# Sliding-window gather on one core: whole 16 KB output rows from two partition halves, with loads of 8 partitions from SyncE and GpSimd

## The chip, the cores and the metric

The kernel runs on one core of one Trainium2 chip. The time is the device time of that core in microseconds (us), the median of several executions. The span of a profiled execution is the time from its first to its last instruction; the time is some 1.7 us longer than the span. Engines are named TensorE (PE), VectorE (DVE), ScalarE (ACT), GpSimd (POOL) and SyncE (SP). The profile counts 16 DMA engines for the core, and all queues share them: from 100 to 160 us 16.2 packets of all queues together are in flight on average before. "The packet records" are the trace's list of every DMA packet with its queue, start, duration and size; they do not name the engine.

## The reference, cut to what matters

```python
batch, c, h, w = (16, 64, 64, 64)          # float32
window_size, stride = 8, 4                 # 15 x 15 windows
for i in range(n_h):
    for j in range(n_w):
        result[:, i, j] = x[:, :, i*4 : i*4+8, j*4 : j*4+8]
# result: (16, 15, 15, 64, 8, 8)
```

There is no arithmetic. Every input row is read once, each inner pixel is written four times: 16.78 MB in, 58.98 MB out.

## The kernel before

Partition = image x channel half x quarter of the rows. Each partition holds 32 channels of 16 image rows, so it can fill four window rows ("slots") of any column of windows; the last slot needs 4 rows of the next quarter, which a shuffle by one partition brings. One window in the output is 16 KB for all channels, so one partition writes 8 KB of it.

```python
L = lpool.tile([P, CL, RB, W], f32)                       # 128 x (32 x 16 x 64)
for k in (2, 0, 1, 3):                                    # quarters of the channels
    for q in range(HQ):
        (nc.sync, nc.scalar)[q % 2].dma_start(out=L[q::HQ, k*cw:(k+1)*cw], in_=x_v[q, :, k*cw:(k+1)*cw, :])
# ... 11 small instructions make the row numbers of the scatters ...
def window(j, s, half):                                   # half: 16 of the 32 channels, or None
    if not last:
        nc.scalar.copy(out=g, in_=L[:, cs, s*ST : s*ST+WS, cols])
    else:
        nc.vector.tensor_copy(out=g[:, :, 0:ST, :], in_=L[:, cs, s*ST:RB, cols])
        nc.vector.stream_shuffle(out=g[:, :, ST:WS, :], in_=L[:, cs, 0:ST, cols], mask=nxt)
    # the last two windows: stores from SyncE; all others: one scatter from GpSimd
    nc.gpsimd.indirect_dma_start(out=o, out_offset=..., in_=g, ...)
# ... the first 8 windows are filled and stored by halves of the channels,
# so that stores are queued before the last quarter of the loads is in ...
```

Of the kernel before, what the change touches and what calls it, by code (L numbers as in the profile page):

```python
# [1 line left out]

# [4 lines left out]


@with_exitstack  # L10
def kernel(
    ctx: ExitStack,
    tc: tile.TileContext,
    x: bass.AP,
    window_size: int,
    stride: int,
    out: bass.AP,
):
    nc = tc.nc
    P = nc.NUM_PARTITIONS  # L20

    B, C, H, W = x.shape
    Bo, NH, NW, Co, WSo, WSo2 = out.shape
    WS = int(window_size)
    ST = int(stride)
    assert Bo == B and Co == C and WSo == WS and WSo2 == WS

    f32 = mybir.dt.float32
    i32 = mybir.dt.int32
    ALU = mybir.AluOpType  # L30
    HQ = 4
    CH = P // (B * HQ)
    CL = C // CH
    RB = H // HQ
    NSLOT = RB // ST
    NWIN = NH * NW
    CFREE = CL * WS * WS
    assert HQ == 4 and CH == 2 and WS == 2 * ST

    lpool = ctx.enter_context(tc.tile_pool(name="lpool", bufs=1))  # L40
    ipool = ctx.enter_context(tc.tile_pool(name="ipool", bufs=1))
    gpool = ctx.enter_context(tc.tile_pool(name="gpool", bufs=1))


    L = lpool.tile([P, CL, RB, W], f32)
    x_v = x.rearrange("b (ch cl) (hq r) w -> hq (b ch) cl (r w)", ch=CH, hq=HQ)
    NCH = 4
    cw = CL // NCH

    for k in (2, 0, 1, 3):  # L50
        for q in range(HQ):
            (nc.sync, nc.scalar)[q % 2].dma_start(
                out=L[q::HQ, k * cw : (k + 1) * cw, :, :],
                in_=x_v[q, :, k * cw : (k + 1) * cw, :],
            )


    def itile(name):
        return ipool.tile([P, 1], i32, name=name)

    pi, tb, tq, tc_, idx, idx_last = (itile(n) for n in ("pi", "tb", "tq", "tc", "idx", "idx_last"))
    nc.gpsimd.iota(pi[:, :], pattern=[[0, 1]], base=0, channel_multiplier=1)  # L62
    nc.vector.tensor_scalar(out=tb[:, :], in0=pi[:, :], scalar1=3, scalar2=None, op0=ALU.logical_shift_right)  # L63
    nc.vector.tensor_scalar(out=tc_[:, :], in0=pi[:, :], scalar1=2, scalar2=1, op0=ALU.logical_shift_right, op1=ALU.bitwise_and)  # L64
    nc.vector.tensor_scalar(out=tq[:, :], in0=pi[:, :], scalar1=HQ - 1, scalar2=None, op0=ALU.bitwise_and)  # L65
    nc.vector.tensor_scalar(out=tb[:, :], in0=tb[:, :], scalar1=float(NWIN * CH), scalar2=None, op0=ALU.mult)  # L66
    nc.vector.tensor_tensor(out=tb[:, :], in0=tb[:, :], in1=tc_[:, :], op=ALU.add)  # L67
    nc.vector.tensor_scalar(out=tc_[:, :], in0=tq[:, :], scalar1=float(NSLOT * NW * CH), scalar2=None, op0=ALU.mult)  # L68
    nc.vector.tensor_tensor(out=idx[:, :], in0=tb[:, :], in1=tc_[:, :], op=ALU.add)  # L69

    nc.vector.tensor_scalar(out=tq[:, :], in0=tq[:, :], scalar1=float(HQ - 1), scalar2=float(2 * B * NWIN * CH), op0=ALU.is_equal, op1=ALU.mult)  # L71
    nc.vector.tensor_tensor(out=idx_last[:, :], in0=idx[:, :], in1=tq[:, :], op=ALU.add)  # L72


    HCL = CL // 2
    idx_h, idx_hlast = itile("idx_h"), itile("idx_hlast")
    for d, e in ((idx_h, idx), (idx_hlast, idx_last)):
        nc.vector.tensor_scalar(out=d[:, :], in0=e[:, :], scalar1=2.0, scalar2=None, op0=ALU.mult)  # L78
    o_v = out.rearrange("b i j (ch cl) r w -> (b i j ch) (cl r w)", ch=CH)
    o_h = out.rearrange("b i j (ch cl) r w -> (b i j ch) (cl r w)", ch=2 * CH)  # L80
    nxt = [min(p + 1, 31) for p in range(32)]

    order = [(j, s) for j in range(NW) for s in range(NSLOT)]


    TAIL, BACK = 2, 3
    o_q = out.rearrange("b i j (ch cl) r w -> i j b ch (cl r w)", ch=CH)

    def free(st):
        tc.declare_no_dep(st.ins, group="stores", reason="each store writes rows of its own")  # L90
        tc.add_to_no_dep_group("stores", st.ins)


    UNITS = 18
    G = [gpool.tile([P, 2 * HCL, WS, WS], f32, name=f"G{n}") for n in range(UNITS // 2)]
    at = 0

    def window(j, s, half):
        nonlocal at
        cols = slice(j * ST, j * ST + WS)  # L100
        last = s == NSLOT - 1
        if half is None:
            n, c0 = 2, 0
            at += at % 2
        else:
            n, c0 = 1, half * HCL
        u = at % UNITS
        at += n
        cs = slice(c0, c0 + n * HCL)
        g = G[u // 2][:, u % 2 * HCL : (u % 2 + n) * HCL, :, :]  # L110
        if not last:
            nc.scalar.copy(out=g, in_=L[:, cs, s * ST : s * ST + WS, cols])  # L112
        else:
            nc.vector.tensor_copy(out=g[:, :, 0:ST, :], in_=L[:, cs, s * ST : RB, cols])  # L114
            nc.vector.stream_shuffle(out=g[:, :, ST:WS, :], in_=L[:, cs, 0:ST, cols], mask=nxt)  # L115
        if (j, s) in order[-TAIL:]:
            g_q = g.rearrange("(m q) c r w -> q m (c r w)", q=HQ)
            for q in range(HQ - 1 if last else HQ):
                free(nc.sync.dma_start(out=o_q[q * NSLOT + s, j], in_=g_q[q]))
            return  # L120
        if half is None:
            o, ix = o_v, (idx_last if last else idx)
        else:
            o, ix = o_h, (idx_hlast if last else idx_h)
        st = nc.gpsimd.indirect_dma_start(  # L125
            out=o,
            out_offset=bass.IndirectOffsetOnAxis(ap=ix[:, 0:1], axis=0),
            in_=g.rearrange("p c r w -> p (c r w)"),
            in_offset=None,
            element_offset=(s * NW + j) * CH * CFREE + (half or 0) * HCL * WS * WS,  # L130
            bounds_check=B * NWIN * CH * (1 if half is None else 2) - 1,
            oob_is_err=False,
        )
        free(st)

    EARLY = 8
    for j, s in order[:EARLY]:
        window(j, s, 0)
    late = list(order[:EARLY])
    rest = list(order[EARLY:])  # L140
    while late:
        for w in late[:2]:
            window(*w, 1)
        for w in rest[:2]:
            window(*w, None)
        late, rest = late[2:], rest[2:]
    for w in rest[:-TAIL]:
        window(*w, None)
    at -= 2 * BACK
    for w in rest[-TAIL:]:  # L150
        window(*w, None)


# [1 line left out]
_INS = ['x', 'window_size', 'stride']  # L155
_OUTS = [((16, 15, 15, 64, 8, 8), 'float32')]

_NUMBERS = {'window_size': 8, 'stride': 4}


# [26 lines left out]
```

## Time and profile before

| | before |
|---|---|
| time, median (lowest to highest) | 193.51 us (193.43 to 193.98) |
| span of the profiled execution | 191.9 us |
| ScalarE / VectorE / GpSimd busy | 45% / 16% / 34% |
| DMA, middle of the run | 405 to 430 GB/s in each slice, no gap |
| scatters, bytes in one | 66, 8 KB a partition (16 of them 4 KB) |

The lines that carry this stand in the prediction below. Read them so: the digits of the DMA row are tenths of the 16 engines' time, one digit a fortieth of the span; if all are 9, only bytes, rate and the two ends can change the time. A compute engine's "idle before, releaser" then tells only that it waits for buffers.

### The profile page before, as it was taken

The numbers are of one execution on the slowest core, as the hardware profiler recorded it, in microseconds if no ns is written. First come the engines' busy times: TensorE is split into PE (matmuls) and PEld (weight loads), VectorE is DVE, ScalarE is ACT, GpSimd is POOL, SyncE is SP. The second block draws the span as 40 slices with busy tenths as digits, with TensorE's granted clock in tenths as the row PEclk, the third lists the DMA queues.
The fourth block names the chain that finished last, engine by engine and source line by source line (L and its number), as shares of the span: only waits on it lengthen the run. The fifth ranks groups of instructions, "written<-read, shape, count | busy, mean of one in ns | idle before, by whom it ended". The sixth has DMA issues, their size and how long they took to land.

```text
span 191.9 us, 458 instructions
## 1 busy us (share of the span) xinstructions
DVE 30.3 (16%) x62; ACT 86.2 (45%) x52; POOL 64.4 (34%) x71
## 2 busy tenths in 40 slices
DVE  2000000402322121211103120303030303000030
ACT  0000000495999646565655656474747473300300
POOL 0000000177877754543434344444444444400000
DMA  5999999999999999999999999999999999999785
GB/s 175 419 412 410 410 410 410 410 410 419 420 430 418 424 415 405 413 412 415 417 418 413 410 412 410 408 406 410 412 413 405 408 405 408 415 413 417 307 277 179
DMA packets 14196, 75.80 MB, mean 395 GB/s; under 512 B 1936, under 2 KB 1936, under 8 KB 7952
## 3 DMA queue, kind: packets, MB, share of 16 engines
q0 software_dynamic: 9504, 57.15, 73.1%
q1 hardware_dynamic: 2512, 10.22, 13.8%
q10 hardware_dynamic: 2176, 8.39, 11.1%
q14 instruction: 4, 0.03, 0.0%
HBM read 16.78 MB, written 62.65 MB: 414 GB/s over the span
## 4 chain that ended last, share of the span: by engine, by line
DMA 66%; issue 25%; POOL 3%; DVE 1%; POOLq 0%; DVEq 0%; PEldq 0%
DMA out_dram<-G,idx 56%; DMA out_dram<-G,idx_h 9%; POOL out_dram L125 3%; DVE G L115 1%; DVE G L114 0%; POOLq L125 0%; POOL pi L62 0%; DVEq L114 0%; PEldq L182 0%
## 5 line engine op out<-in xcount | busy, mean ns | idle before, releaser
L112 ACT COPY G<-L 128x2048 f32<-128x2048 f32 (+1 forms) x51 | 85.0, 1696 | 59.2 <-DMA out_dram<-G,idx_last 25.0
L125 POOL DMA_INDIRECT out_dram<-G,idx x38 | 36.8, 969 | 49.5 <-DMA out_dram<-G,idx 45.6
L114 DVE COPY G<-L 128x1024 f32<-128x1024 f32 (+1 forms) x17 | 11.0, 646 | 152.8 <-DMA out_dram<-G,idx 88.4
L115 DVE STREAM_SHUFFLE G<-L 128x1024 f32<-128x1024 f32 (+1 forms) x17 | 19.5, 1146 | 0.0
L112 ACT ACT_TABLE_LOAD x1 | 1.3, 1283 | 36.3 <-DMA L<-in_x_dram 36.3
L125 POOL DMA_INDIRECT out_dram<-G,idx_hlast x4 | 4.0, 1001 | 37.7 <-DVE G L115 36.8
L125 POOL DMA_INDIRECT out_dram<-G,idx_last x12 | 11.6, 963 | 11.7 <-DVE G L115 7.8
L125 POOL DMA_INDIRECT out_dram<-G,idx_h x12 | 11.7, 975 | 3.7 <-issue 2.4
L63 DVE TENSOR_SCALAR tb<-pi 128x1 int32<-128x1 int32 x1 | 0.2, 153 | 1.0 <-POOL pi L62 1.0
L62 POOL IOTA pi<- 128x1 int32 x1 | 0.1, 119 | 0.4 <-PEq L182 0.4
L115 DVE LOAD_MASK_SELECT G<-L x17 | 0.2, 13 | 0.0
L168 POOL MEMSET const-float32-0.0<- 128x1 f32 x1 | 0.1, 98 | 0.2 <-issue 0.2
L69 DVE CUSTOM_DVE_ANT_0 idx<-tb,tc 128x2 uint16<-128x2 uint16 x1 | 0.2, 161 | 0.0
L67 DVE CUSTOM_DVE_ANT_0 tb<-tb,tc 128x2 uint16<-128x2 uint16 x1 | 0.2, 159 | 0.0
L68 DVE TENSOR_SCALAR tc<-tq 128x1 int32<-128x1 int32 x1 | 0.2, 154 | 0.0
L78 DVE TENSOR_SCALAR idx_hlast<-idx_last 128x1 int32<-128x1 int32 x1 | 0.2, 153 | 0.0
L78 DVE TENSOR_SCALAR idx_h<-idx 128x1 int32<-128x1 int32 x1 | 0.2, 154 | 0.0
L72 DVE CUSTOM_DVE_ANT_0 idx_last<-idx,tq 128x2 uint16<-128x2 uint16 x1 | 0.1, 150 | 0.0
L66 DVE TENSOR_SCALAR tb<-tb 128x1 int32<-128x1 int32 x1 | 0.1, 149 | 0.0
L71 DVE TENSOR_SCALAR tq<-tq 128x1 int32<-128x1 int32 x1 | 0.1, 147 | 0.0
L64 DVE TENSOR_SCALAR tc<-pi 128x1 int32<-128x1 int32 x1 | 0.1, 144 | 0.0
L65 DVE TENSOR_SCALAR tq<-pi 128x1 int32<-128x1 int32 x1 | 0.1, 143 | 0.0
(3 smaller groups left out, 0.3 us busy)
## 6 DMA issues: line engine op xcount, KB each, us to landing
L<-in_x_dram ACTq DMA_DIRECT2D x8, 1024.0 KB, 19.8
L<-in_x_dram SPq DMA_DIRECT2D x8, 1024.0 KB, 20.1
out_dram<-G SPq DMA_DIRECT2D x7, 256.0 KB, 4.1
out_dram<-G,idx POOLq DMA_INDIRECT x38, 18.8
out_dram<-G,idx_h POOLq DMA_INDIRECT x12, 7.0
out_dram<-G,idx_last POOLq DMA_INDIRECT x12, 18.8
out_dram<-G,idx_hlast POOLq DMA_INDIRECT x4, 8.0
```

The source lines that it names most:

```text
L62: nc.gpsimd.iota(pi[:, :], pattern=[[0, 1]], base=0, channel_multiplier=1)
L63: nc.vector.tensor_scalar(out=tb[:, :], in0=pi[:, :], scalar1=3, scalar2=None, op0=ALU.logical_shift_right)
L64: nc.vector.tensor_scalar(out=tc_[:, :], in0=pi[:, :], scalar1=2, scalar2=1, op0=ALU.logical_shift_right, op1=ALU.bitwise_and)
L65: nc.vector.tensor_scalar(out=tq[:, :], in0=pi[:, :], scalar1=HQ - 1, scalar2=None, op0=ALU.bitwise_and)
L67: nc.vector.tensor_tensor(out=tb[:, :], in0=tb[:, :], in1=tc_[:, :], op=ALU.add)
L68: nc.vector.tensor_scalar(out=tc_[:, :], in0=tq[:, :], scalar1=float(NSLOT * NW * CH), scalar2=None, op0=ALU.mult)
L69: nc.vector.tensor_tensor(out=idx[:, :], in0=tb[:, :], in1=tc_[:, :], op=ALU.add)
L78: nc.vector.tensor_scalar(out=d[:, :], in0=e[:, :], scalar1=2.0, scalar2=None, op0=ALU.mult)
L112: nc.scalar.copy(out=g, in_=L[:, cs, s * ST : s * ST + WS, cols])
L114: nc.vector.tensor_copy(out=g[:, :, 0:ST, :], in_=L[:, cs, s * ST : RB, cols])
L115: nc.vector.stream_shuffle(out=g[:, :, ST:WS, :], in_=L[:, cs, 0:ST, cols], mask=nxt)
L125: st = nc.gpsimd.indirect_dma_start(out=o, out_offset=bass.IndirectOffsetOnAxis(ap=ix[:, 0:1], axis=0), in_=g.rearrange("p c r w -> p (c r ...
```

## The change

Its intent: let each store packet be a whole 16 KB row, so that the fixed cost of a packet and of a scatter (4 ns and some 55 ns by the records of before, as the prediction works out) is paid half as often, and let stores begin when half of the images (y = 0) are in. The channel halves move to the two partition halves; the lower 64 partitions collect one slot, the upper 64 the next, and each buffer is filled from both halves by copies that shift by 64 partitions. The loads go by 8 partitions.

```diff
-    HQ = 4
-    CH = P // (B * HQ)
+    CH = 2
+    HQ = P // (B * CH)
...
-    for k in (2, 0, 1, 3):
+    SMALL = 4
+    for y in range(NY):
         for q in range(HQ):
-            (nc.sync, nc.scalar)[q % 2].dma_start(...)          # 32 partitions
+            load(nc.sync, 0, y, q, SMALL, CL)                   # 8 partitions each
+            load(nc.gpsimd, 0, y, q, 0, SMALL)
+            load(nc.gpsimd, 1, y, q, 0, CL)
...
+    for t in range(NG): ...                                     # zero what early scatters drop
+            nc.vector.memset(G[t][p0 : p0 + QP, :, :, :], 0.0)
+    for y in range(NY):                                         # early: columns 0 to 2, slots 0/1
+        for j in range(EARLY):
+            for half in range(CH):
+                fill(G[t % NG], half, half, j, y * QP, QP, (act, dve))
+            scatter(G[t % NG], (idx_y0, idx_y1)[y], j, 0)
...
+        if s == 0:                                              # slots 0 and 1
+            for half in range(CH):
+                fill(g, half, s + half, j, 0, HP, (act, dve))
+            scatter(g, idx, j, s)
+        else:                                                   # slots 2 and 3
+            turn = j % 2
+            fill(g, turn, s, j, 0, HP, (act, act))
+            fill(g, 1 - turn, s + 1, j, 0, HP, (dve, dve))
+            scatter(g, (idx_hi, idx_lo)[turn], j, s)
```

`fill` makes two copies, one from the partitions' own half of the channels and one from the other half. A "unit" below is one buffer's worth: four such copies and the scatter that stores it. The row numbers for the scatters take 21 small instructions on VectorE; they stand after the loads in the program text.

More of the change, by code (lines that the diff above doesn't have):

```diff
@@ L36 @@
     NWIN = NH * NW
-    CFREE = CL * WS * WS
-    assert HQ == 4 and CH == 2 and WS == 2 * ST
+    CFREE = C * WS * WS
+    HP = P // CH
+    YB = 8
+    NY = B // YB
+    QP = YB * HQ
+    assert HQ == 4 and WS == 2 * ST and QP == 32 and NSLOT == 4
     lpool = ctx.enter_context(tc.tile_pool(name="lpool", bufs=1))
@@ L45, with load @@
     L = lpool.tile([P, CL, RB, W], f32)
-    x_v = x.rearrange("b (ch cl) (hq r) w -> hq (b ch) cl (r w)", ch=CH, hq=HQ)
-    NCH = 4
-    cw = CL // NCH
-    for k in (2, 0, 1, 3):
+    x_v = x.rearrange("(y b) (ch cl) (hq r) w -> ch y hq b cl (r w)", y=NY, ch=CH, hq=HQ)
+    SMALL = 4
+    def load(eng, ch, y, q, c0, c1):
+        p0 = ch * HP + y * QP + q
+        eng.dma_start(out=L[p0 : p0 + QP - HQ + 1 : HQ, c0:c1, :, :], in_=x_v[ch, y, q, :, c0:c1, :])
+    for y in range(NY):
         for q in range(HQ):
-            (nc.sync, nc.scalar)[q % 2].dma_start(
-                out=L[q::HQ, k * cw : (k + 1) * cw, :, :],
-                in_=x_v[q, :, k * cw : (k + 1) * cw, :],
-            )
+            load(nc.sync, 0, y, q, SMALL, CL)
+            load(nc.gpsimd, 0, y, q, 0, SMALL)
+            load(nc.gpsimd, 1, y, q, 0, CL)
@@ L58, in itile @@
     def itile(name):
         return ipool.tile([P, 1], i32, name=name)
-    pi, tb, tq, tc_, idx, idx_last = (itile(n) for n in ("pi", "tb", "tq", "tc", "idx", "idx_last"))
+    pi, tb, tq, tc_, th, idx, idx_y0, idx_y1, idx_lo, idx_hi = (
+        itile(n) for n in ("pi", "tb", "tq", "tc", "th", "idx", "idx_y0", "idx_y1", "idx_lo", "idx_hi")
+    )
+    FAR = float(2 * B * NWIN)
     nc.gpsimd.iota(pi[:, :], pattern=[[0, 1]], base=0, channel_multiplier=1)
-    nc.vector.tensor_scalar(out=tb[:, :], in0=pi[:, :], scalar1=3, scalar2=None, op0=ALU.logical_shift_right)
@@ L64 @@
-    nc.vector.tensor_scalar(out=tc_[:, :], in0=pi[:, :], scalar1=2, scalar2=1, op0=ALU.logical_shift_right, op1=ALU.bitwise_and)
-    nc.vector.tensor_scalar(out=tq[:, :], in0=pi[:, :], scalar1=HQ - 1, scalar2=None, op0=ALU.bitwise_and)
-    nc.vector.tensor_scalar(out=tb[:, :], in0=tb[:, :], scalar1=float(NWIN * CH), scalar2=None, op0=ALU.mult)
-    nc.vector.tensor_tensor(out=tb[:, :], in0=tb[:, :], in1=tc_[:, :], op=ALU.add)
-    nc.vector.tensor_scalar(out=tc_[:, :], in0=tq[:, :], scalar1=float(NSLOT * NW * CH), scalar2=None, op0=ALU.mult)
@@ L69 @@
-    nc.vector.tensor_tensor(out=idx[:, :], in0=tb[:, :], in1=tc_[:, :], op=ALU.add)
-    nc.vector.tensor_scalar(out=tq[:, :], in0=tq[:, :], scalar1=float(HQ - 1), scalar2=float(2 * B * NWIN * CH), op0=ALU.is_equal, op1=ALU.mult)
-    nc.vector.tensor_tensor(out=idx_last[:, :], in0=idx[:, :], in1=tq[:, :], op=ALU.add)
-    HCL = CL // 2
-    idx_h, idx_hlast = itile("idx_h"), itile("idx_hlast")
-    for d, e in ((idx_h, idx), (idx_hlast, idx_last)):
-        nc.vector.tensor_scalar(out=d[:, :], in0=e[:, :], scalar1=2.0, scalar2=None, op0=ALU.mult)
@@ L79 @@
-    o_v = out.rearrange("b i j (ch cl) r w -> (b i j ch) (cl r w)", ch=CH)
-    o_h = out.rearrange("b i j (ch cl) r w -> (b i j ch) (cl r w)", ch=2 * CH)
-    nxt = [min(p + 1, 31) for p in range(32)]
-    order = [(j, s) for j in range(NW) for s in range(NSLOT)]
-    TAIL, BACK = 2, 3
-    o_q = out.rearrange("b i j (ch cl) r w -> i j b ch (cl r w)", ch=CH)
-    def free(st):
-        tc.declare_no_dep(st.ins, group="stores", reason="each store writes rows of its own")
-        tc.add_to_no_dep_group("stores", st.ins)
@@ L94 @@
-    UNITS = 18
-    G = [gpool.tile([P, 2 * HCL, WS, WS], f32, name=f"G{n}") for n in range(UNITS // 2)]
-    at = 0
-    def window(j, s, half):
-        nonlocal at
-        cols = slice(j * ST, j * ST + WS)
-        last = s == NSLOT - 1
-        if half is None:
-            n, c0 = 2, 0
-            at += at % 2
-        else:
-            n, c0 = 1, half * HCL
-        u = at % UNITS
-        at += n
-        cs = slice(c0, c0 + n * HCL)
-        g = G[u // 2][:, u % 2 * HCL : (u % 2 + n) * HCL, :, :]
-        if not last:
-            nc.scalar.copy(out=g, in_=L[:, cs, s * ST : s * ST + WS, cols])
-        else:
-            nc.vector.tensor_copy(out=g[:, :, 0:ST, :], in_=L[:, cs, s * ST : RB, cols])
-            nc.vector.stream_shuffle(out=g[:, :, ST:WS, :], in_=L[:, cs, 0:ST, cols], mask=nxt)
-        if (j, s) in order[-TAIL:]:
-            g_q = g.rearrange("(m q) c r w -> q m (c r w)", q=HQ)
-            for q in range(HQ - 1 if last else HQ):
-                free(nc.sync.dma_start(out=o_q[q * NSLOT + s, j], in_=g_q[q]))
-            return
-        if half is None:
-            o, ix = o_v, (idx_last if last else idx)
-        else:
-            o, ix = o_h, (idx_hlast if last else idx_h)
@@ new lines, in bits, with mul, tt @@
+    def bits(d, shift, mask):
+        nc.vector.tensor_scalar(out=d[:, :], in0=pi[:, :], scalar1=shift, scalar2=mask, op0=ALU.logical_shift_right, op1=ALU.bitwise_and)
+    def mul(d, a, m):
+        nc.vector.tensor_scalar(out=d[:, :], in0=a[:, :], scalar1=float(m), scalar2=None, op0=ALU.mult)
+    def tt(d, a, b, op):
+        nc.vector.tensor_tensor(out=d[:, :], in0=a[:, :], in1=b[:, :], op=op)
+    bits(tb, 2, B - 1)
+    bits(tq, 0, HQ - 1)
+    bits(tc_, 6, 1)
+    mul(tb, tb, NWIN)
+    mul(th, tq, NSLOT * NW)
@@ new lines @@
+    tt(tb, tb, th, ALU.add)
+    mul(th, tc_, NW)
+    tt(idx, tb, th, ALU.add)
+    bits(th, 5, 1)
+    mul(th, th, FAR)
+    tt(idx_y0, idx, th, ALU.add)
+    nc.vector.tensor_scalar(out=th[:, :], in0=th[:, :], scalar1=-1.0, scalar2=FAR, op0=ALU.mult, op1=ALU.add)
+    tt(idx_y1, idx, th, ALU.add)
+    nc.vector.tensor_scalar(out=tq[:, :], in0=tq[:, :], scalar1=float(HQ - 1), scalar2=FAR, op0=ALU.is_equal, op1=ALU.mult)
+    tt(th, tc_, tq, ALU.mult)
+    tt(idx_hi, idx, th, ALU.add)
+    nc.vector.tensor_scalar(out=tc_[:, :], in0=tc_[:, :], scalar1=-1.0, scalar2=1.0, op0=ALU.mult, op1=ALU.add)
@@ L125, in window, with scatter @@
+    tt(th, tc_, tq, ALU.mult)
+    tt(idx_lo, tb, th, ALU.add)
+    mul(th, tc_, NW)
+    tt(idx_lo, idx_lo, th, ALU.add)
+    o_v = out.rearrange("b i j c r w -> (b i j) (c r w)")
+    nxt = [min(p + 1, 31) for p in range(32)]
+    NG = 4
+    G = [gpool.tile([P, C, WS, WS], f32, name=f"G{n}") for n in range(NG)]
+    def scatter(g, ix, j, s):
         st = nc.gpsimd.indirect_dma_start(
-            out=o,
+            out=o_v,
             out_offset=bass.IndirectOffsetOnAxis(ap=ix[:, 0:1], axis=0),
@@ L129, in window @@
             in_offset=None,
-            element_offset=(s * NW + j) * CH * CFREE + (half or 0) * HCL * WS * WS,
-            bounds_check=B * NWIN * CH * (1 if half is None else 2) - 1,
+            element_offset=(s * NW + j) * CFREE,
+            bounds_check=B * NWIN - 1,
             oob_is_err=False,
         )
-        free(st)
-    EARLY = 8
-    for j, s in order[:EARLY]:
-        window(j, s, 0)
-    late = list(order[:EARLY])
-    rest = list(order[EARLY:])
-    while late:
-        for w in late[:2]:
-            window(*w, 1)
-        for w in rest[:2]:
-            window(*w, None)
-        late, rest = late[2:], rest[2:]
@@ L147, with fill @@
-    for w in rest[:-TAIL]:
-        window(*w, None)
-    at -= 2 * BACK
-    for w in rest[-TAIL:]:
-        window(*w, None)
+        tc.declare_no_dep(st.ins, group="stores", reason="each store writes rows of its own")
+        tc.add_to_no_dep_group("stores", st.ins)
+    def fill(g, half, s, j, lo, n, copies):
+        d = slice(half * HP + lo, half * HP + lo + n)
+        cols = slice(j * ST, j * ST + WS)
+        for ch in (half, 1 - half):
+            f = slice(ch * HP + lo, ch * HP + lo + n)
+            cs = slice(ch * CL, (ch + 1) * CL)
+            copy = copies[ch != half]
+            if s < NSLOT - 1:
+                copy(out=g[d, cs, :, :], in_=L[f, :, s * ST : s * ST + WS, cols])
+            else:
+                copy(out=g[d, cs, 0:ST, :], in_=L[f, :, s * ST : RB, cols])
+                nc.vector.stream_shuffle(out=g[d, cs, ST:WS, :], in_=L[f, :, 0:ST, cols], mask=nxt)
@@ new lines @@
+    act, dve = nc.scalar.copy, nc.vector.tensor_copy
+    EARLY = 3
+    assert EARLY < NG
+    for t in range(NG):
+        for half in range(CH):
+            p0 = half * HP + (QP if t < EARLY else 0)
+            nc.vector.memset(G[t][p0 : p0 + QP, :, :, :], 0.0)
+    t = 0
+    for y in range(NY):
[3 more added lines that the diff above has]
+            scatter(G[t % NG], (idx_y0, idx_y1)[y], j, 0)
+            t += 1
@@ new lines @@
+    units = [(j, s) for j in range(NW) for s in (0, 2) if s or j >= EARLY]
+    for j, s in units:
+        g = G[t % NG]
+        t += 1
+        if s == 0:
+            for half in range(CH):
+                fill(g, half, s + half, j, 0, HP, (act, dve))
+            scatter(g, idx, j, s)
+        else:
+            turn = j % 2
+            fill(g, turn, s, j, 0, HP, (act, act))
+            fill(g, 1 - turn, s + 1, j, 0, HP, (dve, dve))
+            scatter(g, (idx_hi, idx_lo)[turn], j, s)
```

## The prediction

> **What bounds the kernel now.** I read the busy shares by engine first, then the row of DMA activity over 40 slices, then the table of stretches, then the groups of instructions by form, and last the chain of waits and the timeline near the end. Shares and slices:
>
> ```profile
> DVE 30.3 (16%) x62; ACT 86.2 (45%) x52; POOL 64.4 (34%) x71
> ...
> DMA  5999999999999999999999999999999999999785
> GB/s 175 419 412 410 410 410 410 410 410 419 420 430 418 424 415 405 413 412 415 417 418 413 410 412 410 408 406 410 412 413 405 408 405 408 415 413 417 307 277 179
> ```
>
> No compute engine is busy even half of the time, and DMA is full in every slice but the first and the last three. The kernel is a copy: 16.78 MB in, and 16 x 15 x 15 x 64 x 64 x 4 bytes = 58.98 MB out, 75.76 MB together. At 410 GB/s that is 184.8 us of a 191.9 us span; the other 7 us are the start and the tail. A slice is 4.8 us, so the first loses (410-175)/410 x 4.8 = 2.8 us and the last three lose (103+133+231)/410 x 4.8 = 5.5 us. The stretches:
>
> ```profile
> 30.00:60.00 30.00, 6.05 (x15) 21.34 (x18) 17.12 (x18) 1.00 1.03 417
> 60.00:90.00 30.00, 5.94 (x9) 19.37 (x11) 16.16 (x17) 1.00 1.02 415
> 90.00:120.00 30.00, 5.68 (x9) 17.07 (x9) 11.56 (x12) 1.00 1.01 412
> ```
>
> Columns: stretch, length, busy time and count of VectorE, ScalarE and GpSimd, clock, DMA share, GB/s. The first has the hand-over from loads to stores in it (loads end near 45 us) and shows no gap: copies of 16 channels, ready when half of a quarter-sliced load is there, put stores in the queues (GpSimd's first at 37.7 us) before the loads run out. That is the thing to keep in mind for the change.
>
> Durations that I shall reuse:
>
> ```profile
> L112 ACT COPY G<-L 128x2048 f32<-128x2048 f32 x39 | 73.8, 1897 | 56.9 <-DMA out_dram<-G,idx_last 25.0 <-DMA out_dram<-G,idx 17.1 <-DVE G L115 13.3
> L125 POOL DMA_INDIRECT out_dram<-G,idx x38 | 36.8, 969 | 49.5 <-DMA out_dram<-G,idx 45.6 <-issue 2.8 <-ACT G L112 1.1
> L115 DVE STREAM_SHUFFLE G<-L 128x1024 f32<-128x1024 f32 x13 | 16.6, 1278 | 0.0
> L114 DVE COPY G<-L 128x1024 f32<-128x1024 f32 x13 | 9.3, 715 | 105.9 <-DMA out_dram<-G,idx 88.4 <-DMA out_dram<-G,idx_h 9.6 <-ACT G L112 7.9
> L114 DVE COPY G<-L 128x512 f32<-128x512 f32 x4 | 1.7, 422 | 46.9 <-DMA L<-in_x_dram 41.4 <-DMA out_dram<-G,idx_h 5.5
> ```
>
> The copies wait for stores (buffers), not the other way round. The tail in the timeline:
>
> ```profile
> 166.62 0.96 POOL L125 DMA_INDIRECT out_dram<-G,idx  x1 [1.73 <-DMA out_dram<-G,idx]
> 179.87 1.90 ACT L112 COPY G<-L 128x2048 f32<-128x2048 f32 x1 [14.74 <-DMA out_dram<-G,idx_last]
> 181.79 5.67 SPq L119 DMA_DIRECT2D out_dram<-G  x7
> ```
>
> The last two windows are filled late and stored from SyncE while the GpSimd queue runs dry. The trace's packet records show why: from 180 to 183 us only 8 of the 16 DMA engines still have store packets; these 8 lag by about 3.5 us. The same records say when they fall behind: in stretches without a scatter being issued an 8 KB packet takes 314 ns on average, in those with one 325 to 335 ns with single ones near 400. 3.5 us over 66 scatters is some 55 ns each. With half the engines idle a packet takes 309 ns, a 4 KB packet 159.
>
> [...]
>
> **The change, part by part.**
>
> *Bytes.* The same 75.76 MB, so a DMA floor of about 184 us stays. All gain must come from time per byte, the start or the tail.
>
> *Row size.* Stores go from 8 KB to 16 KB rows. In the records successive 4 KB packets of an engine start 155 ns apart, 8 KB ones 306: a fixed part of 4 ns. A 16 KB row then costs 608 instead of 612, 0.7%. With all engines working it is 2 x 311 - 4 = 618.
>
> *Scatters.* 66 become 33 (six half ones for 3 columns x 2 image halves, 12 pairs of slots 0/1, 15 pairs of slots 2/3). The lag of the slow engines halves, from 3.5 to about 1.8 us. But the dropped rows now fall on one half of the partitions at a time[...]. Store phase of the lower engines: 226 x 618 = 139.7, plus 33 x 80 ns of lag and completion = 2.6: about 142.3 us.
>
> *Loads.* 16.78 MB. [...]256 packets of 4 KB at 155-160 ns = 40 to 41 us. Starting at 2.2 us (the first load packet of before)[...], they end at 43 to 44.
>
> *Where the early stores go.* The intent is plain: image half y=0 is loaded by about 23 us, its copies fill three buffers, and stores could begin at 25 us. But in the order of instructions as built, VectorE executes 8 memsets, 6 copies for y=0, **two copies that wait for the y=1 loads**, and only then the 21 small index instructions. The first scatter needs the index tile of y=0, the twelfth of these. VectorE is in order, so no scatter leaves before all loads are in. ([...]6 copies of 1.3 us, from 422 and 715 ns extrapolated to 2048 elements, end near 42.6 us: hidden, just.) So at the hand-over: loads end 43.8, semaphore 0.75 (before: last load packet 44.97, VectorE starts 45.74), copies 1.3 to 2.6, twelve index instructions 1.4 (before: eleven from 0.98 to 2.34), GpSimd's start 0.3, first data 1.3 (SyncE's store at the tail: issue 181.79, packet 183.10). First store packet at about 50 us. DMA is **idle for some 6 us** where before had no gap.
>
> *Ramp.* Four half scatters (2.55 us of DMA each) follow 1.27 us apart and end at 60.2. A buffer is refilled by two ScalarE copies of 1.9 us, so ScalarE gives a unit every 3.8 us; the fifth and sixth are in time, the seventh (ready 64.7, data 66.3, queue dry at 65.3) leaves a hole of about 1 us. After that each unit is 4 to 5 us of DMA against 3.8 of ScalarE, or 2 x (0.7 + 1.28) = 4.0 of VectorE, and four 2 MB buffers hold 15 us of pending work. Compute is hidden: ScalarE 66 x 1.9 = 125 us in all.
>
> *Tail.* No queue change at the end; both halves finish together but for about 2 rows (1.2 us, counted), then 1.3 us to the span's end as before (190.59 to 191.9).
>
> Sum: 50 + 142.3 + 1 + 1.3 = 194.6 us of span. The measured time of before is 1.65 over its span (193.55 against 191.9), so 196.2. In differences: tail and lag gain 4 to 5, row size under 1, hand-over loses 6 to 7, ramp 1.
>
> **Rivals.** *A, the early stores work*: no idle hand-over, stores mixed with loads. Then 43 + 142.3 + 2 + 1.3 + 1.65 = about 190. For it speaks that the whole kernel is laid out for it; against it the order on VectorE, which I take as decisive. *B, the 16 KB rows stream distinctly better*, at the 309 ns per 8 KB that half-idle engines show: 226 x 614 + 2.6 = 141.4, one us less; even without lag it gives 193 to 195. A real jump is not to be seen: the stretch with many 4 KB rows (45 to 90 us) ran at 418 GB/s, that with 8 KB rows alone (90 to 178 us) at 411. [...]*D, compute becomes the bound*: [...]in the steady state it needs 6.6 us per two units against 10 of DMA, so only if shifted copies cost half as much again. Then 205.
>
> **Range and chances.** Store phase 139 to 145 and first store at 48 to 53 us span most of the doubt: 191.5 to 201.5. Two per cent are 189.7 and 197.4. Faster needs A and a better rate, 0.06. The upper limit is only 1.2 us above my figure, so slower gets 0.36, the same 0.58.
>
> **What would show it.** Right: a trough in the DMA row at 44 to 50 us, first scatter of GpSimd at 48 to 49 behind VectorE's index instructions, 410 to 420 GB/s after it, and no low slices but the last. Wrong: scatters at 25 us (A), store slices above 425 (B), 200 GB/s during the loads (C), or dips in mid-run with waits of scatters for VectorE or ScalarE (D).

Rival C: loads on half of the engines at half of 410 GB/s, some 80 us, and a time near 235. The 256 packets of the loads are 16.78 MB in packets of 4 KB, shared evenly by 16 engines. The 226 rows of "the lower engines" are 6 x 4 + 12 x 8 + 8 x 8 + 7 x 6 rows, for eight engines that write the partition half with fewer dropped rows; the other eight have 224. That a half falls on eight engines was an assumption. The changed kernel's records bear it out: of the first scatter of slots 2 and 3, which drops 16 rows of one half, 4-byte packets come eight at 72.99, 16 at 74.83 and eight at 76.00 us, 16 for the dropped rows and 16 more, and 1.85 us are three rows of 618 ns. Of the 80 ns for each scatter 55 are the lag worked out above; the rest was my estimate. The 42.6 us have a memset time in them; in rival D "it" is VectorE.

## The result, and the profile after

The changed kernel takes 203.58 us (203.29 to 203.67), the kernel before 193.51. The ratio is 1.0513 (95% interval 1.0493 to 1.0533). Here and below a ratio is the mean time of one kernel's runs over that of the other's of the same rounds, so it isn't quite the ratio of the medians quoted. Executions over 1.5% slower than the fastest of the same kernel are left out of the means. I had forecast 196.2 with a range of 191.5 to 201.5: the direction was within what I allowed, the size was not.

The page of the changed kernel, busy times and the 40 slices (now 5.05 us each):

```profile
DVE 131.2 (65%) x155; ACT 125.5 (62%) x67; POOL 52.6 (26%) x54
...
DMA  2999999993299899999999999999999999999980
GB/s 93 337 406 399 401 399 400 398 397 98 104 409 406 330 390 412 409 422 416 414 416 429 430 416 416 419 416 432 425 419 416 416 422 432 425 419 414 416 373 36
```

The DMA row of this page has a hole that the row of before has not: 98 and 104 GB/s in the two slices from 45 to 56 us. The loads before it run at 400 where before had 410, the stores after it at 414 to 432 where before had 405 to 418, and the slices at both ends are lower. The stretches (columns: stretch, length, busy time and count of VectorE, ScalarE, GpSimd, clock, DMA share, GB/s), first of before, then of after:

```profile
5.00:40.00 35.00, 2.00 (x6) 3.69 (x4) 1.99 (x2) 1.00 1.03 411
90.00:178.00 88.00, 15.19 (x24) 43.63 (x23) 30.82 (x32) 1.00 1.01 411
```

```profile
5.00:45.00 40.00, 31.27 (x14) 12.27 (x7) 7.46 (x12) 1.00 1.03 392
90.00:180.00 90.00, 58.81 (x74) 73.77 (x41) 25.78 (x20) 1.00 1.01 421
```

Loads lost 5% of their rate (in part because GpSimd's begin late, at 5.06 us), stores won 2.4%. By these rates the 58.98 MB of stores gain 143.5 - 140.1 = 3.4 us, and the 16.78 MB of loads lose 42.8 - 40.8 = 2.0.

The hole, in the timeline of after (start, length, engine, what, count, and in brackets how long the engine had waited and for what):

```profile
35.67 6.93 DVE L136 COPY G<-L 32x2048 f32<-32x2048 f32 x6
...
48.04 2.47 DVE L136 COPY G<-L 32x2048 f32<-32x2048 f32 x2 [5.44 <-issue]
50.54 0.15 DVE L77 TENSOR_SCALAR tb<-pi 128x1 int32<-128x1 int32 x1
...
51.93 0.16 DVE L83 CUSTOM_DVE_ANT_0 idx_y<-idx,th 128x2 uint16<-128x2 uint16 x1
...
52.77 0.15 DVE L103 TENSOR_SCALAR tc<-tc 128x1 int32<-128x1 int32 x1
52.95 1.07 POOL L115 DMA_INDIRECT out_dram<-G,idx_y  x1 [16.09 <-DVE tc L103]
```

By 42.6 us VectorE has filled three buffers with rows of y = 0. They are ready to store, but the row numbers come at 52 us: VectorE stops before the two copies for y = 1 (they start at 48.04; the profile names no releaser, but the last load packet has ended at 47.24) and makes its row numbers only after them. GpSimd waited 16 us for them.

The groups of instructions that answer to those shown of before:

```profile
L136 ACT COPY G<-L 64x2048 f32<-64x2048 f32 (+1 forms) x66 | 124.2, 1896 | 28.9 <-DMA out_dram<-G,idx 10.1
L136 DVE COPY G<-L 64x2048 f32<-64x2048 f32 (+1 forms) x36 | 43.9, 1227 | 22.8 <-DMA out_dram<-G,idx 12.7
L139 DVE STREAM_SHUFFLE G<-L 64x1024 f32<-64x1024 f32 x30 | 38.3, 1276 | 0.0
L150 DVE MEMSET G<- 32x4096 f32 x8 | 27.8, 3472 | 8.0 <-issue 5.4
L115 POOL DMA_INDIRECT out_dram<-G,idx x12 | 13.8, 1149 | 34.7 <-ACT G L136 29.2
L115 POOL DMA_INDIRECT out_dram<-G,idx_hi x8 | 11.7, 1459 | 31.1 <-DVE G L139 17.9
```

A copy to shifted partitions costs what an unshifted one of as many elements a partition did (1896 against 1897 ns on ScalarE, whose 66 copies, shifted or not, all take 1888 to 1902), and half-filled lanes (64 of 128 partitions) save nothing. That doubles the copying, and yet compute isn't the bound: the copies still wait for stores.

From the packet records I worked out where DMA engines stood idle: the sum, over the time, of the engines below 16 that have a packet in flight, divided by 16. This gives the ledger of the 9.9 us between the spans:

| us of full DMA lost, or time | before | after | difference |
|---|---|---|---|
| start, 0 to 8 us | 2.44 | 3.90 | +1.46 |
| hand-over from loads to stores, 44 to 56 us | 0.00 | 7.61 | +7.61 |
| ramp after it, 56 to 90 us | 0.01 | 1.76 | +1.75 |
| uneven ends of the engines, from 170 us to the last store packet | 2.84 | 1.77 | -1.07 |
| last store packet to the end of the span | 1.32 | 3.26 | +1.94 |
| the rest, engines working | 185.3 | 183.5 | -1.8 |
| span | 191.9 | 201.8 | +9.9 |

The ramp is the stretch of the first scatters, before the copies have run ahead of the stores. The idea of the change is in the last line but one and is worth 1.8 us net of slower loads; another 1.1 us comes from ends that are less uneven. The other lines are what it costs to start, hand over and end.

### The profile page after: what moved, and what is told of

The parts are those of the page before. It is cut to its first block, busy times and chain, and to the rows that moved or that the text cites. A ratio compares the mean times of both kernels' runs of the same rounds, so it can differ in the third digit from the quotient of the medians.

```text
span 201.8 us, 478 instructions
## 1 busy us (share of the span) xinstructions
DVE 131.2 (65%) x155; ACT 125.5 (62%) x67; POOL 52.6 (26%) x54
## 3 DMA queue, kind: packets, MB, share of 16 engines
HBM read 16.78 MB, written 69.21 MB: 426 GB/s over the span
## 4 chain that ended last, share of the span: by engine, by line
DMA 65%; issue 8%; DVE 7%; ACT 7%; POOL 3%; POOLq 1%; DVEq 0%; PEldq 0%; ACTq 0%
DMA out_dram<-G,idx 20%; DMA L<-in_x_dram 16%; DMA out_dram<-G,idx_hi 14%; DMA out_dram<-G,idx_lo 12%; ACT G L136 7%; DVE G L136 4%; DMA out_dram<-G,idx_y 3%; POOL L L57 2%; DVE G L139 2%; POOL out_dram L115 1%; DVE G L138 1%; POOLq L203 1%; DVE th L80 0%; DVE idx_y L83 0%; POOLq L115 0%
## 5 line engine op out<-in xcount | busy, mean ns | idle before, releaser
L136 ACT COPY G<-L 64x2048 f32<-64x2048 f32 (+1 forms) x66 | 124.2, 1896 | 28.9 <-DMA out_dram<-G,idx 10.1
L136 DVE COPY G<-L 64x2048 f32<-64x2048 f32 (+1 forms) x36 | 43.9, 1227 | 22.8 <-DMA out_dram<-G,idx 12.7
L139 DVE STREAM_SHUFFLE G<-L 64x1024 f32<-64x1024 f32 x30 | 38.3, 1276 | 0.0
L138 DVE COPY G<-L 64x1024 f32<-64x1024 f32 x30 | 20.7, 691 | 21.4 <-DMA out_dram<-G,idx_hi 14.4
L150 DVE MEMSET G<- 32x4096 f32 x8 | 27.8, 3472 | 8.0 <-issue 5.4
L115 POOL DMA_INDIRECT out_dram<-G,idx x12 | 13.8, 1149 | 34.7 <-ACT G L136 29.2
L115 POOL DMA_INDIRECT out_dram<-G,idx_hi x8 | 11.7, 1459 | 31.1 <-DVE G L139 17.9
L57 POOL DMA_DIRECT2D L<-in_x_dram x16 | 9.9, 625 | 25.2 <-DMA L<-in_x_dram 24.3
L115 POOL DMA_INDIRECT out_dram<-G,idx_lo x7 | 8.9, 1278 | 18.8 <-ACT G L136 9.7
L115 POOL DMA_INDIRECT out_dram<-G,idx_y x6 | 6.9, 1152 | 22.9 <-DVE tc L103 16.1
```

Source lines behind the costliest of these rows:

```text
L57: eng.dma_start(out=L[p0 : p0 + QP - HQ + 1 : HQ, c0:c1, :, :], in_=x_v[ch, y, q, :, c0:c1, :])
L115: st = nc.gpsimd.indirect_dma_start(out=o_v, out_offset=bass.IndirectOffsetOnAxis(ap=ix[:, 0:1], axis=0), in_=g.rearrange("p c r w -> p (c ...
L136: copy(out=g[d, cs, :, :], in_=L[f, :, s * ST : s * ST + WS, cols])
L138: copy(out=g[d, cs, 0:ST, :], in_=L[f, :, s * ST : RB, cols])
L139: nc.vector.stream_shuffle(out=g[d, cs, ST:WS, :], in_=L[f, :, 0:ST, cols], mask=nxt)
L150: nc.vector.memset(G[t][p0 : p0 + QP, :, :, :], 0.0)
```

## The experiments

All of them are correct in their results. The kernel before ran on the same chips and took 193.33 to 193.60 us in each group.

### The row numbers first

```diff
+    # the whole of "itile ... idx_lo" moved here, ahead of the loads
     for y in range(NY):
         for q in range(HQ):
             load(nc.sync, 0, y, q, SMALL, CL)
```

> Only the order of the program text changes: the index tiles are computed ahead of the loads and so stand ahead of every copy on VectorE. Theory 1 (the 7 us of idle DMA at the hand-over come from the index instructions standing behind copies that wait for the y=1 loads): the first scatter moves from 52.9 us to about 42 us (VectorE still has the memsets and four copies before it), the idle stretch from 47.2 to 54.6 us is gone, and the time falls by about 7 us, from 203.6 to 196 to 197 us. Rival (the hand-over is set by copies and buffers, and the index chain is only its own 2 us): 201 to 202 us, and an idle stretch of 4 us or more stays.

Measured: 197.7 us (197.63 to 197.87), ratio to before 1.023 (1.0207 to 1.0252). That is 5.9 us below the changed kernel. The DMA and GB/s rows of its page:

```profile
DMA  2999999999987789999999999999999999999980
GB/s 82 341 397 402 402 399 397 399 399 402 422 358 313 321 358 395 425 425 413 422 428 428 423 415 425 425 428 425 415 412 422 422 422 425 412 422 427 428 375 30
```

The hole is gone: by the ledger 0.3 us instead of 7.6 is lost from 44 to 56 us. It is theory 1, and the size is what it said but for 1 us (the first scatter is issued at 44.54 us, not at about 42), because the ramp behind it got worse (3.6 us lost from 56 to 90, against 1.8). The rival, a hand-over set by buffers, would have left 4 us of idle time.

But the stores did not begin early either. The first packet of that scatter comes at 46.65, when the loads are nearly done (47.42).

### The row numbers first, and half of the memsets on ScalarE

```diff
+            if half:
+                nc.scalar.copy(out=G[t][p0 : p0 + QP], in_=zero[p0 : p0 + QP, 0:1] ... )
+            else:
                 nc.vector.memset(G[t][p0 : p0 + QP, :, :, :], 0.0)
```

> The index tiles first, as in the run of that name, and half of the memsets on ScalarE, so that both engines are free when the loads of y=0 land near 29 us. Theory 6 (what bounds the hand-over once the index chain is out of the way is that GpSimd's queue holds the y=1 loads ahead of the scatters[...], and ScalarE's 3.8 us a unit after it): the first scatter is issued at 34 to 36 us instead of 44.5, but the time moves by less than 1 us from 197.7. Rival (the memsets on VectorE are what keeps rival A of the prediction from coming true): 194 us or less.

Measured: 197.87 us (197.81 to 197.88), the same as without the split memsets: theory 6. The first scatter is issued 7 us sooner, if 1.3 us later than I had put it, as its timeline shows (start, length, engine, what):

```profile
37.31 1.38 POOL L115 DMA_INDIRECT out_dram<-G,idx_y  x1 [0.92 <-ACT G L136]
```

Its first packet still comes at 46.74 us, and the loads end at 47.25. So it is neither the row numbers nor the memsets that keep stores from mixing with loads: the first packet of a scatter that GpSimd issues behind its own loads comes 9.4 us after it. In the kernel before, where GpSimd has no loads, the first store packet comes at 42.09 us, 4.4 us after its scatter is issued and 2.9 us before the last load packet has ended. That the scatter waits behind the loads in GpSimd's own queue is my reading of these times. The packet records show one more thing. In GpSimd's queue of the changed kernel stand 3712 packets of 4 bytes. Counted as 16 for each scatter and load they make 49 x 16 = 784, as one for each dropped row 624 (the same count gives all 1568 of the kernel before, 66 x 16 + 512); that leaves 2304, exactly as many as GpSimd's loads have packets of 4 KB. They come at the pace of these packets (some 50 in a microsecond while the loads run, 250 and more in the last two) and speed up just when SyncE's last loads end (45.46 us in this run). What they are for, and whether the scatters wait for them, is not shown.

### The memsets alone on ScalarE

```diff
-            nc.vector.memset(G[t][p0 : p0 + QP, :, :, :], 0.0)
+            nc.scalar.copy(out=G[t][p0 : p0 + QP] ..., in_=zero[p0 : p0 + QP, 0:1] ... )
```

(Two builds simply left the memsets out; a scatter then reads partitions that nothing has written.)

> Only the eight memsets move from VectorE to ScalarE, which is idle then. In the changed kernel GpSimd starts issuing at 1.38 us, but the first packet of its loads comes at 5.06 us. Theory 2a[...]: the first packet comes near 3 us, the loads end 2 us earlier, and the time falls to 201 to 202 us. Theory 2b (the start is GpSimd's own): first packet stays near 5 us, load end near 47 us and time within 0.5 us of 203.6. The index chain stays behind the y=1 copies either way.

Measured: 203.42 us (203.35 to 203.9). The first packet of GpSimd's loads comes at 4.79 us instead of 5.06, and the loads end at 47.52. By theory 2a VectorE's memsets hold GpSimd's loads up; with the memsets on ScalarE the first packet came only 0.27 us sooner, so it is 2b. Why GpSimd's loads take 3.7 us from the first issue (1.38) to the first packet (5.06), when its first scatter takes 1.64 us (52.95 to 54.59), stays open.

### No small loads

```diff
-            load(nc.sync, 0, y, q, SMALL, CL)
-            load(nc.gpsimd, 0, y, q, 0, SMALL)
+            load(nc.sync, 0, y, q, 0, CL)
             load(nc.gpsimd, 1, y, q, 0, CL)
```

> Only the loads change: no small 4-channel loads; SyncE loads all 32 channels of the lower half, GpSimd only the 1 MB loads of the upper half. Theory 7[...]: [...]loads end at 62 to 68 us and the time is 219 to 226 us. Rival (the engines follow the partitions): 202 to 204 us, loads end near 47 us as before.

Measured: 227.4 us (two runs, 227.39 and 227.42), 1.4 us more than the range I had given; the loads end at 71.6 us, not at 62 to 68. The DMA and GB/s rows of its page, a slice being 5.6 us:

```profile
DMA  3999995555553199899999999999999999999991
GB/s 107 291 275 297 358 278 205 203 210 209 209 210 126 46 392 398 353 404 410 392 424 433 421 417 418 420 418 421 433 424 421 418 418 418 418 430 421 426 395 73
```

From 34 to 71 us half of the DMA engines work, at half the rate (203 to 210 GB/s in full slices). In the changed kernel SyncE's loads of 8 partitions, while they run alone from 3 to 5 us, have 8.1 packets in flight on average, and from 10 to 45 us SyncE's have 7.2 and GpSimd's 8.9. Theory 7 was that without the small loads half of GpSimd's large loads fall on the eight engines that SyncE's use. If all of GpSimd's loads went to the same 8 engines as SyncE's, the changed kernel's loads could not have ended at 47 us (16.78 MB at the 205 GB/s of these slices would take some 80 us, an estimate). Without the small loads, then, a part of rival C of the prediction comes true: for some 37 us half of the engines do the loading. Which loads share engines, and how the small loads prevent it, is not shown, since the records do not name the engine. GpSimd's queue has 2048 of the unexplained 4-byte packets in this run, again as many as its loads have packets of 4 KB (8 x 256). What my range had left out is the stretch before 34 us, where all 16 engines have packets but move only 304 GB/s (10 to 25 us); why is not shown.

### Loads from SyncE and ScalarE alone

```diff
-            load(nc.sync, 0, y, q, SMALL, CL)
-            load(nc.gpsimd, 0, y, q, 0, SMALL)
-            load(nc.gpsimd, 1, y, q, 0, CL)
+    for c in (0, CL // 2):
+        for q in range(HQ):
+            for ch in range(CH):       # 16 partitions, 16 channels each
+                (nc.sync, nc.scalar)[ch].dma_start(out=L[ch*HP + q : (ch+1)*HP : HQ, c : c + CL//2], in_=x_h[ch, q, :, c : c + CL//2, :])
```

> Only the loads change: SyncE loads the lower half of the partitions and ScalarE the upper, 16 partitions and 16 channels each, none from GpSimd. Theory 3 (the loads of the changed kernel end 3 us late because GpSimd's start at 5.06 us and carry one 4-byte packet for each 4 KB packet): these packets are gone from the GpSimd queue, the loads end at 44 to 45 us as in the kernel before, the hand-over stays idle for some 7 us, and the time is 200.5 to 201.5 us. Rival 3b[...]: packets of 4 KB take well over 165 ns, the loads end at 50 us or later, and the time is over 206 us.

Measured: 209.81 and 211.43 us in two runs; the other two, 214.66 and 216.17, are slow. The 4-byte packets are gone as expected: 1152 stay in GpSimd's queue, 33 x 16 + 624. But the 4 KB packets take 193 ns on average where the changed kernel has 167 to 170 and before 162 to 166; the loads end at 51.1 us. The outcome is that of rival 3b (packets well over 165 ns, the loads end after 50 us, a time over 206). Part of the loss is a thing I had not counted: with both image halves in each load, ScalarE can't copy any rows of y = 0 during the loads, and the ramp loses 7.9 us in place of 1.8. Why these packets are slower no run here isolates. So this layout of channel halves leaves poor choices for loads: 8 partitions from SyncE keep only 8 engines busy (in the changed kernel 8.1 packets are in flight on average from 3 to 5 us, when SyncE's loads run alone), so the upper half comes from GpSimd, and loads of 16 partitions ran slower (193 ns a packet). Since the slow packets cover everything else, the run doesn't show what the late start and the 4-byte packets of the changed kernel's loads cost: theory 3 stays untested.

### Two scatters of 8 KB rows in place of one of 16 KB

```diff
+        for ch in range(CH):
             st = nc.gpsimd.indirect_dma_start(
-                out=o_v, ... in_=g.rearrange("p c r w -> p (c r w)"),
+                out=o_h, ... in_=g[:, ch*CL : (ch+1)*CL].rearrange("p c r w -> p (c r w)"),
```

> Each scatter of 16 KB rows becomes two of 8 KB rows, 66 in all as in the kernel before; nothing else changes. Theory 4 (the store phase is faster than before, 421 against 411 GB/s, because there are half as many scatters and packets): 226 rows on the slower engines lose 14 ns each, 3.2 us, so 206 to 207.5 us, and store slices return to about 411 GB/s. Rival (the better store rate comes from something else, such as the copies' order or the spread over engines): within 1 us of 203.6.

Measured: 212.9 us (212.78 to 213.24), 9.3 us more than the changed kernel, not 3.2. The direction of theory 4 is right, and the store rate returns to that of before and a little below it. First the group of its scatters (columns: line, engine, operation, count, busy us, mean ns, idle before and releasers), then the stretch from 90 to 180 us with columns as above:

```profile
L123 POOL DMA_INDIRECT out_dram<-G,twice x66 | 88.4, 1340 | 66.3 <-DMA out_dram<-G,twice 17.6 <-ACT G L144 17.6 <-DVE th L83 16.1
```

```profile
90.00:180.00 90.00, 58.69 (x75) 70.22 (x37) 51.77 (x38) 1.00 1.01 408
```

It is 408 GB/s here against 421. The ledger splits the 9.3 us: 4.1 in the working time (two packets of 8 KB take 2 x 321.6 = 643 ns, one of 16 KB 624.7), 2.8 more lost in the ramp, 0.9 more in the uneven ends, 1.3 more after the last packet, 0.3 at the hand-over (0.1 less at the start). I had counted only the first. So larger rows in fewer scatters are the good part of this change. Whether the rows' size or the number of scatters brings it, this run can't tell, since it changes both.

### The last unit from SyncE

```diff
-            scatter(g, (idx_hi, idx_lo)[turn], j, s)
+            if (j, s) == units[-1]:
+                store_sp(g, j, s)          # 7 stores of 16 partitions
+            else:
+                scatter(g, (idx_hi, idx_lo)[turn], j, s)
```

> Only the last unit changes: seven stores of 16 partitions from SyncE in place of the last scatter. Theory 5 (the 3.2 us from the last store packet to the end of the span, against 1.3 us in the kernel before, are GpSimd finishing its own queue after a late scatter): the end comes 1.3 to 1.5 us after the last packet, and the time falls by 1 to 1.8 us, to 201.8 to 202.6. Rival (the wait is for the data of any queue): 3 us stay, and the time is 203.5 or more, since 16-partition stores run less evenly than a scatter.

Measured: 204.81 us (204.69 to 205.03), 1.2 us more than the changed kernel: a miss. The packets of SyncE's 16-partition stores take 875 ns on average, against 625, and the last one comes 2.6 us later (201.23 against 198.59). In the kernel before, too, the packets of SyncE's stores took longer on average, 404 ns against 319 for the scatters' packets of the same 8 KB.

From the last store packet to the end of the span it takes 2.0 us instead of 3.3, but nothing was won there. The last long instruction to end, in the changed kernel and in this run, is one of GpSimd at the end of the program, its DRAIN. Its lines in before, the changed kernel and this run (line, engine, operation, count, shortest/median/longest ns, first and last start; the first start belongs to the longest):

```profile
L182 POOLq DRAIN  x3: 40/108/21710, 166.4 to 191.6; - x3
L203 POOLq DRAIN  x3: 51/105/16648, 184.4 to 201.6; - x3
L216 POOLq DRAIN  x3: 51/105/23283, 179.2 to 203.0; - x3
```

It ends at 188.10, 201.05 and 202.45 us, that is 3.07, 2.47 and 2.54 us after the last store packet of GpSimd's own queue (185.04, 198.58, 199.91). In every variant of the changed kernel the span ends 0.8 us after this DRAIN; in before it is done 2.5 us before SyncE's last store packet has ended (190.59). How long it runs on after the last packet of GpSimd's queue goes, in the five runs compared, with the number of DMAs that GpSimd has issued: 1.75 us with 33 (no loads from GpSimd), 2.14 with 41 (no small loads), 2.47 with 49, 3.07 with 66 (before), 3.72 with 82 (two scatters for one), some 0.04 us each. What it does in this time is not shown. So theory 5 fits, but a store from SyncE behind a scatter that ends as late as 199.91 us didn't avoid it.

### Everything together, and without the stores from SyncE

```diff
     # row numbers first, memsets split, and:
-            turn = j % 2
+            turn = (j + 1) % 2             # lower half 224 rows, not 226
+                # some early y = 1 units: ScalarE 1 copy, VectorE 3
+                fill(..., (dve, dve) if y and half and j % 2 else (act, dve))
+            # last unit: store_sp, in the first of the two runs only
```

> Everything that the earlier runs point to: index first, memsets split, one more copy of some early y=1 units on VectorE, slots 2/3 turned so that the lower partitions write 224 rows instead of 226, the last unit from SyncE. If each keeps its worth: 197.7 less 1 to 2 for the ramp, 1 to 1.8 for the tail, 0.6 for the rows: 193 to 195 us, about level with the kernel before (193.4) and not below it by 2%. It would be under 191 only if the ramp after the loads vanished.

Measured: 197.47 us (197.16 to 197.57), ratio 1.0199 (1.0177 to 1.0221): no better than the row numbers alone, and above my 193 to 195. The ramp lost 0.8 us instead of 3.6, but the stores from SyncE took it back (packets of 779 ns).

> The combined kernel without its stores from SyncE: index first, memsets split, two of the three early y=1 units with three copies on VectorE and one on ScalarE, slots 2/3 turned the other way. In the run with everything the ramp between 56 and 90 us lost 0.8 us of DMA in place of 3.6, but its last unit from SyncE cost about 2 us (packets of 779 ns against 624). Theory 8 (so the two cancelled, and ScalarE's pace of 3.8 us a unit is what the ramp costs): 194 to 195.5 us, 2 to 3.5 us under the run with the index first alone. Rival (the ramp's gain is given back later): 197 us or more. Neither is below the kernel before (193.5) by 2%.

Measured, with two such units (j even) instead of one: 195.74 us (195.59 to 195.81), ratio 1.0112 (1.0084 to 1.014). It is just above the range of theory 8, and the gain over the row numbers alone is 2.0 us. By the ledger 1.7 us of it come from the ramp (1.9 lost instead of 3.6) and 0.6 from more even ends (1.0 instead of 1.5, with the slots turned), while the hand-over loses 0.5 more. So not all of the ramp's gain is kept: hand-over and ramp together lost 1.5 us in the run with everything and 2.7 here. One such unit with the last scatter left in place was not run. This is the best variant that I found of the changed kernel. It is 7.8 us faster than the changed kernel and, by 1.1%, still slower than the kernel before. I found none that beats both. The DMA and GB/s rows of its page:

```profile
DMA  2999999999989799999999999999999999999990
GB/s 89 334 399 404 401 401 395 400 401 403 426 328 377 328 432 378 432 426 410 432 415 404 429 432 429 412 426 422 412 412 432 432 422 412 422 419 407 429 432 30
```

What is left against before shows in these two rows: the first slices (GpSimd's late start), 400 instead of 411 GB/s during the loads, dips in the ramp, and the last slice.

## Why the prediction was wrong, point by point

The mechanism at the hand-over was right. Four terms of the sum were too small, most of all the end of the loads, and behind one of them, the tail, stood a wrong assumption. Measured less predicted is 203.6 - 196.2 = 7.4 us.

- **"In the order of instructions as built, VectorE executes ... two copies that wait for the y=1 loads, and only then the 21 small index instructions": right.** The order settled it, not the intent in the text, and moving the index instructions is worth 5.9 us.
- **"They end at 43 to 44" (the loads): wrong by 3.4 us, the largest term.** They end at 47.24. I had let GpSimd's loads begin little later than SyncE's 2.2 us, on no measurement; their first packet comes at 5.06. I had counted 155 to 160 ns a packet; SyncE's take 169.7 ns on average, GpSimd's 167.4. SyncE's loads last 45.47 - 2.30 = 43.2 us. At 256 packets an engine (4096 on 16, an estimate, since the records do not name the engine) this is 169 ns each; what part of it the 4-byte packets of GpSimd's queue cost no run isolates. The end at 47.24 is that of GpSimd's loads: 47.24 - 5.06 = 42.2 us, by the same estimate 165 ns each. My 43.8 less 256 packets of 159 ns leaves 3.1 us for their start. So of the 3.4 us some 1.9 are the late start and 1.5 the slower packets. What causes either stays open.
- **"First store packet at about 50 us": 54.59.** Of the 4.6 us, 3.4 are the loads. The chain from the last load to the first store took 7.35 us instead of 6.2: both copies come after the loads (2.47 us), GpSimd is released by the seventeenth small instruction (L103), not by the twelfth, and its first packet takes 1.64 us instead of 1.3.
- **"Store phase of the lower engines ... about 142.3 us", and a hole of "about 1 us" in the ramp: nearly right.** From first to last store packet it is 144.0 us, of which 1.8 are the ramp. Packets of 16 KB have a median of 618 ns, the very figure used (their mean is 624.7). So the gain of the whole rows had the right size, and was too small for what it had to pay.
- **"1.3 us to the span's end as before": wrong by 2.0 us.** It is 3.26 us. Before ends with stores from SyncE, some 5.5 us after the last packet of its GpSimd queue; the changed kernel ends with a scatter, and GpSimd's DRAIN comes after that (2.47 us, then 0.8 to the end). I had carried the tail over from a kernel that ends on another queue. In the prediction's differences this stands as "tail and lag gain 4 to 5": by the ledger the uneven ends gained 1.1 and the tail lost 1.9.
- The four terms, 3.4 + 1.15 + 0.7 + 1.96, give 7.2 us; the rest is the difference between span and time (1.74 us in place of 1.65, with rounding).
- **Hidden memsets, "just": right.** They repeat every 4.38 us (1.65, 6.04, 10.41 us), 3.47 of it busy and 0.91 idle; VectorE's early copies end at 42.6 us, as forecast. In this there is luck: the six copies took 6.9 us instead of 7.8, and the memsets, whose time no trace of before showed, 35.0.
- **Rival A, "the early stores work", about 190 us: false for a second reason that I did not see.** Even with the row numbers first and the first scatter issued at 37.31 us, its first packet came at 46.74, when GpSimd's loads were nearly out of its queue (47.25).
- **Rival B** was as small as I put it (421 GB/s from 90 to 180 us, single slices up to 432), and **D** didn't come: ScalarE and VectorE are busy 62% and 65% and their dips are in the ramp alone. GpSimd's scatters took 1149 and 1459 ns instead of 969, which costs nothing in mid-run.

The range was too narrow because I let the doubt sit in the store phase and the order, and gave the loads and the tail, which I had taken over from the kernel before, none.

## What to carry to other kernels

When DMA is full from end to end, a change is paid for at the start, the hand-over and the end (here 1.5 us, 9.4 with the ramp, and 0.9, for 1.8 gained in the middle): work out these three as carefully as the middle, and take none of them over from a kernel that uses other queues there. Read the built order of each in-order engine before believing in an early start, and ask what else is ahead in the queue that the first store will use. A load shape that suits the buffers may keep only some of the DMA engines busy, as SyncE's loads of 8 partitions did with 8.1 packets in flight; count the packets in flight, by queue.
